# Row softmax on one core: the load of the fifth chunk issued as two DMAs of eight rows

## Chip, core and metric

The kernel runs on one core of one Trainium2 chip. The metric is the device time of one execution in microseconds (us). The kernel before took 161.8 us, the median of 3 runs (161.76 to 161.93). The profiled execution spans 160.5 us from its first to its last instruction.

## The reference

The input is an array of 16 x 1024 rows of 512 float32 numbers, 33.55 MB; the output has the same shape. Each row goes through a softmax with temperature 0.5:

```python
temp = 0.5
x_scaled = x / temp
x_max = np.max(x_scaled, axis=-1, keepdims=True)
exp_x = np.exp(x_scaled - x_max)
return (exp_x / np.sum(exp_x, axis=-1, keepdims=True)).astype(np.float32)
```

Every number is read once and written once, so 67.1 MB pass through the DMA engines.

## The kernel before, in words

The 16,384 rows are cut into C = 8 chunks of 2,048 rows. In a chunk each of the 128 partitions holds G = 16 rows that lie next to each other in DRAM, so a partition's share of a chunk is one contiguous run of 32 KiB, and a chunk is 4 MiB. `xt` is the tile of a chunk; there are `BUFS = 6` of them. Chunks 0 to 5 have a buffer each; chunk 6 takes the buffer of chunk 0 and chunk 7 that of chunk 1, so their loads must wait until the stores of chunks 0 and 1 are done. Everything happens in place: the exponentials and the scaled results overwrite the input in `xt`.

Three lists say how the work is cut. `LOADS` (L38) lists, for each chunk, the row ranges of its load DMAs: chunk 0 in two (rows 0 to 4 and 4 to 16), chunks 1 to 6 whole, chunk 7 without its last row. `BLOCKS` (L39) lists the row ranges for the computation: chunk 0 in three blocks, chunks 1 to 6 in one block, chunk 7 in two, 11 blocks in all. `STORES` (L40) stores each chunk whole, after its last block.

For a block `i` these steps are taken:

- `shift(i)`: if the chunk's load has not been issued yet, `load` issues it on SyncE's DMA queue (L68, queue q1 in the profile). VectorE takes the negated maximum of each row (L77, `negmax`) and doubles it (L81, `bias`).
- `exponentials(i)`: ScalarE computes exp(2x + bias) a row at a time and sums the row in the same instruction (L108).
- `scale_vector(i)`: VectorE takes the reciprocals of the sums (L125) and multiplies seven eighths of the rows by them (L127).
- `scale_scalar(i)`: ScalarE multiplies the other rows (L138).
- `store(i)`: ScalarE issues the store (L148, queue q10).

The order on each engine is written out by hand: the loop at the end of the kernel does, for each `i`, the exponentials of block `i + 1`, the scaling of block `i`, the maximum of block `i + 2` and the store of block `i`. VectorE thus alternates between the maximum of one chunk and the scaling of the one two before it. SyncE issues the loads of chunks 0 to 5 in the first microseconds, and they stand in its queue one behind the other.

The last row of each partition's share of chunk 7 goes another way: `load_last_row` issues it on GpSimd's queue (L97, q0) once ScalarE is at row 10 of chunk 5. A list named `finished` collects DMAs and last instructions for which SyncE waits at the very end (L174).

Of the kernel before, what the change touches and what calls it, by code (L numbers as in the profile page):

```python
# [1 line left out]

# [4 lines left out]


@with_exitstack
def kernel(  # L10
    ctx: ExitStack,
    tc: tile.TileContext,
    x: bass.AP,
    out: bass.AP,
):
    nc = tc.nc
    fp32 = mybir.dt.float32
    P = nc.NUM_PARTITIONS
    AX = mybir.AxisListType.X
    EXP = mybir.ActivationFunctionType.Exp  # L20
    COPY = mybir.ActivationFunctionType.Copy
    MAX = mybir.AluOpType.max

    D = x.shape[-1]
    xf = x.flatten_outer_dims()
    of = out.flatten_outer_dims()
    N = xf.shape[0]

    G = 16
    C = N // (P * G)
    assert C * P * G == N
    xr = xf.rearrange("(c p g) d -> c p g d", p=P, g=G)
    outr = of.rearrange("(c p g) d -> c p g d", p=P, g=G)
    WHOLE = [(0, G)]
    LOADS = [[(0, 4), (4, G)]] + [WHOLE] * 6 + [[(0, G - 1)]]  # L38
    BLOCKS = [[(0, 4), (4, 8), (8, G)]] + [WHOLE] * 6 + [[(0, 8), (8, G)]]  # L39
    STORES = [WHOLE] * 8  # L40
    BMAX = 16
    BUFS = 6

    data = ctx.enter_context(tc.tile_pool(name="data", bufs=BUFS))
    stats = ctx.enter_context(tc.tile_pool(name="stats", bufs=6))

    ctx.enter_context(tc.manual_schedule())


    warm = stats.tile([P, 1], fp32, name="warm", bufs=1)  # L50
    nc.vector.memset(warm, 0.0)  # L51
    nc.scalar.activation(out=warm, in_=warm, func=EXP)  # L52

    chunks = {}
    blocks = [(c, lo, hi) for c in range(C) for lo, hi in BLOCKS[c]]
    n = len(blocks)
    biases, sums, recips = {}, {}, {}

    finished = []

    def load(c):
        if c < BUFS:
            chunks[c] = data.tile([P, G, D], fp32, name="xt")
        else:
            chunks[c] = chunks[c - BUFS]
        xt = chunks[c]
        for lo, hi in LOADS[c]:
            part = nc.sync.dma_start(out=xt[:, lo:hi, :], in_=xr[c][:, lo:hi, :])  # L68
            finished.append(part.ins.name)

    def shift(i):
        c, lo, hi = blocks[i]
        if c not in chunks:
            load(c)
        b = hi - lo
        negmax = stats.tile([P, BMAX], fp32, name="negmax")
        nc.vector.tensor_reduce(  # L77
            negmax[:, 0:b], chunks[c][:, lo:hi, :], axis=AX, op=MAX, negate=True
        )
        biases[i] = stats.tile([P, BMAX], fp32, name="bias")  # L80
        nc.vector.tensor_scalar_mul(biases[i][:, 0:b], negmax[:, 0:b], 2.0)  # L81

    def load_last_row(signal):
        seen = stats.tile([P, 1], fp32, name="seen", bufs=1)
        copied = nc.gpsimd.tensor_copy(out=seen, in_=signal)  # L90
        finished.append(copied.ins.name)
        c = C - 1
        halves = "p (h d) -> p h d"
        to = chunks[c - BUFS][:, G - 1, :].rearrange(halves, h=2)
        of_ = xr[c][:, G - 1, :].rearrange(halves, h=2)
        for p0, p1 in ((P - 2, P), (0, P - 2)):
            part = nc.gpsimd.dma_start(  # L97
                out=to[p0:p1], in_=of_[p0:p1], max_dma_last_dim=2 * D
            )
            finished.append(part.ins.name)  # L100

    def exponentials(i, rows):
        c, lo, hi = blocks[i]
        if i not in sums:
            sums[i] = stats.tile([P, BMAX], fp32, name="sums")
        for g in rows:
            row = chunks[c][:, lo + g, :]
            nc.scalar.activation(  # L108
                out=row,
                in_=row,  # L110
                func=EXP,
                bias=biases[i][:, g : g + 1],
                scale=2.0,
                accum_out=sums[i][:, g : g + 1],
            )
            if c == BUFS - 1 and g == 10:
                load_last_row(sums[i][:, g : g + 1])


    def scale_vector(i):  # L120
        c, lo, hi = blocks[i]
        b = hi - lo
        k = b - b // 8
        recips[i] = stats.tile([P, BMAX], fp32, name="recip")
        nc.vector.reciprocal(recips[i][:, 0:b], sums[i][:, 0:b])  # L125
        rows = chunks[c][:, lo : lo + k, :]
        last = nc.vector.tensor_mul(  # L127
            rows, rows, recips[i][:, 0:k].unsqueeze(2).broadcast_to((P, k, D))
        )
        if i == n - 1:  # L130
            finished.append(last.ins.name)

    def scale_scalar(i):
        c, lo, hi = blocks[i]
        b = hi - lo
        for g in range(b - b // 8, b):
            row = chunks[c][:, lo + g, :]
            last = nc.scalar.activation(  # L138
                out=row, in_=row, func=COPY, scale=recips[i][:, g : g + 1]
            )  # L140
            if i == n - 1:
                finished.append(last.ins.name)

    def store(i):
        c, _, end = blocks[i]
        for lo, hi in STORES[c]:
            if hi == end:
                part = nc.scalar.dma_start(  # L148
                    out=outr[c][:, lo:hi, :], in_=chunks[c][:, lo:hi, :]
                )  # L150
                if c < C - 1:
                    finished.append(part.ins.name)

    shift(0)
    shift(1)

    def rows(i):
        c, lo, hi = blocks[i]
        cut = hi - lo - (2 if c == 1 else 0)
        return range(cut), range(cut, hi - lo)  # L160

    exponentials(0, rows(0)[0])
    for i in range(n):
        if i + 1 < n:
            exponentials(i + 1, rows(i + 1)[0])
        scale_vector(i)
        scale_scalar(i)
        if i + 2 < n:
            shift(i + 2)
        store(i)  # L170
        if i + 1 < n:
            exponentials(i + 1, rows(i + 1)[1])

    seen = nc.sync.nop()  # L174
    info = mybir.DependencyInfo(
        mybir.DependencyClass.Sync, mybir.DependencyReason.DATA
    )
    for name in finished:
        tc.add_manual_dep(seen.ins, name, info, reason="leaves one wait for the end")


# [1 line left out]
_INS = ['x']  # L183
_OUTS = [((16, 1024, 512), 'float32')]


# [23 lines left out]
```

## Time and profile before

| What | Number |
|---|---|
| time, median of 3 | 161.8 us |
| span of the profiled execution | 160.5 us |
| VectorE (DVE) busy | 134.6 us, 84% |
| ScalarE (ACT) busy | 102.2 us, 64% |
| DMA | 67.13 MB, mean 418 GB/s |
| maxima on VectorE (L77) | 11, together 69.9 us |
| scaling on VectorE (L127) | 11, together 62.0 us |
| exponentials on ScalarE (L108) | 128, together 90.4 us |
| stores (L148) | 8 of 4,096 KB, median 23.1 us from issue to landing |

A profile line of part 2 cuts the span into 40 slices of 4.0 us; each digit is the busy share of a slice in tenths. In part 3 a line gives a DMA queue, its packets, its MB and the share of the time of the 16 DMA engines that its packets took. A group of instructions reads: line, engine, operation, output and input, count, then busy time and the mean of one in ns, then the idle time ahead of them with what ended most of it. In a list of waits the numbers are total, count and longest. A line of DMA issues ends with the time from issue to landing. In a list by time the first number is the start, the second the duration.

A "piece" below is the contiguous run of one partition in one DMA, which the trace records as one packet: 32 KiB for a whole chunk.

### The profile page before, as it was taken

How to read it: one execution, taken by the hardware profiler on the slowest of the kernel's cores; microseconds unless marked ns; L12 is line 12 of the kernel's file. 1: busy time of each engine (PE TensorE's matmuls, PEld its weight loads, DVE VectorE, ACT ScalarE, POOL GpSimd, SP SyncE). 2: the span in 40 equal slices, each digit the busy share in tenths (PEclk: the TensorE clock that was granted, in tenths of full speed). 3: DMA queues.
4: the chain of work that ended last, by engine and by line, in shares of the span. 5: the costliest groups of instructions: out<-in, count | busy, mean ns of one | idle time of the engine just before them, and what ended most of it. 6: DMA issues, size and time to landing. Idle time of an engine off the chain costs nothing.

```text
span 160.5 us, 411 instructions
## 1 busy us (share of the span) xinstructions
DVE 134.6 (84%) x45; ACT 102.2 (64%) x273; POOL 1.9 (1%) x7
## 2 busy tenths in 40 slices
DVE  0607999999999999999999999999999999957000
ACT  3071549069989963998199909991899891790000
POOL 0000000000000000000000000030000000000000
DMA  5999999999989999999999999989999999999994
GB/s 184 470 408 498 400 392 457 457 392 402 506 269 425 490 392 400 506 400 392 490 425 392 474 434 392 490 383 483 422 450 400 400 465 441 392 457 449 400 441 204
DMA packets 2578, 67.13 MB, mean 418 GB/s; under 512 B 328, under 2 KB 328, under 8 KB 400
## 3 DMA queue, kind: packets, MB, share of 16 engines
q1 hardware_dynamic: 1296, 33.29, 49.3%
q10 hardware_dynamic: 1152, 33.55, 48.4%
q0 software_dynamic: 128, 0.26, 0.4%
q14 instruction: 2, 0.02, 0.0%
HBM read 33.55 MB, written 33.55 MB: 418 GB/s over the span
## 4 chain that ended last, share of the span: by engine, by line
DVE 75%; DMA 7%; issue 5%; ACT 3%; SPq 0%
DVE negmax L77 42%; DVE xt L127 31%; DMA xt<-in_x_dram 7%; ACT xt L108 3%; DVE bias L81 1%; DVE recip L125 1%; SPq L68 0%
## 5 line engine op out<-in xcount | busy, mean ns | idle before, releaser
L108 ACT ACTIVATE xt<-xt,bias 128x512 f32<-128x512 f32 x128 | 90.4, 708 | 41.5 <-DVE bias L81 40.6
L77 DVE TENSOR_REDUCE negmax<-xt 128x16 f32<-128x8192 f32 (+2 forms) x11 | 69.9, 6352 | 9.4 <-DMA xt<-in_x_dram 9.4
L127 DVE TENSOR_TENSOR xt<-xt,recip 128x7168 f32<-128x7168 f32 (+2 forms) x11 | 62.0, 5637 | 0.4
L108 ACT ACTIVATION_READ_ACCUMULATOR xt<-xt,bias 128x1 f32 x128 | 23.9, 187 | 0.0
L138 ACT ACTIVATE xt<-xt,recip 128x512 f32<-128x512 f32 x15 | 9.9, 706 | 0.0
L125 DVE RECIPROCAL recip<-sums 128x16 f32<-128x16 f32 (+2 forms) x11 | 2.4, 218 | 1.8 <-ACT xt L108 1.8
L81 DVE TENSOR_SCALAR bias<-negmax 128x16 f32<-128x16 f32 (+2 forms) x11 | 1.9, 173 | 0.4
L52 ACT ACT_TABLE_LOAD x1 | 1.3, 1283 | 0.7 <-PEq L194 0.7
L97 POOL DMA_DIRECT2D xt<-in_x_dram x2 | 1.5, 741 | 0.5 <-issue 0.5
L90 POOL COPY seen<-sums 128x1 f32<-128x1 f32 x1 | 0.2, 184 | 103.6 <-ACT xt L108 103.6
L51 DVE MEMSET warm<- 128x1 f32 x1 | 0.1, 59 | 0.8 <-PEq L194 0.8
L52 ACT ACTIVATE warm<-warm 128x1 f32<-128x1 f32 x1 | 0.2, 202 | 0.0
L194 POOL MEMSET const-float32-0.0<- 128x1 f32 x1 | 0.1, 93 | 0.2 <-issue 0.2
L194 POOL MEMSET const-bfloat16-1.0<- 128x1 bf16 x1 | 0.1, 95 | 0.0
L194 POOL MEMSET const-uint8-127<- 128x1 uint8 x1 | 0.1, 95 | 0.0
L194 POOL MEMSET const-float32-1.0<- 128x1 f32 x1 | 0.1, 93 | 0.0
## 6 DMA issues: line engine op xcount, KB each, us to landing
out_dram<-xt ACTq DMA_DIRECT2D x8, 4096.0 KB, 23.1
xt<-in_x_dram SPq DMA_DIRECT2D x6, 4096.0 KB, 34.8
xt<-in_x_dram SPq DMA_DIRECT2D x1, 3840.0 KB, 27.8
xt<-in_x_dram SPq DMA_DIRECT2D x1, 3072.0 KB, 11.6
xt<-in_x_dram SPq DMA_DIRECT2D x1, 1024.0 KB, 4.8
xt<-in_x_dram POOLq DMA_DIRECT2D x1, 252.0 KB, 15.4
xt<-in_x_dram POOLq DMA_DIRECT2D x1, 4.0 KB, 9.1
```

The source lines that it names most:

```text
L51: nc.vector.memset(warm, 0.0)
L52: nc.scalar.activation(out=warm, in_=warm, func=EXP)
L77: nc.vector.tensor_reduce(negmax[:, 0:b], chunks[c][:, lo:hi, :], axis=AX, op=MAX, negate=True)
L81: nc.vector.tensor_scalar_mul(biases[i][:, 0:b], negmax[:, 0:b], 2.0)
L90: copied = nc.gpsimd.tensor_copy(out=seen, in_=signal)
L97: part = nc.gpsimd.dma_start(out=to[p0:p1], in_=of_[p0:p1], max_dma_last_dim=2 * D)
L108: nc.scalar.activation(out=row, in_=row, func=EXP, bias=biases[i][:, g : g + 1], scale=2.0, accum_out=sums[i][:, g : g + 1],)
L125: nc.vector.reciprocal(recips[i][:, 0:b], sums[i][:, 0:b])
L127: last = nc.vector.tensor_mul(rows, rows, recips[i][:, 0:k].unsqueeze(2).broadcast_to((P, k, D)))
L138: last = nc.scalar.activation(out=row, in_=row, func=COPY, scale=recips[i][:, g : g + 1])
L194: nc = _bacc.Bacc("TRN2", target_bir_lowering=False, num_devices=1)
```

## The change

The load of the fifth chunk (index 4) is issued as two DMAs of eight rows each, one behind the other on the same queue. The pieces are then 16 KiB instead of 32 KiB. Each DMA has its own semaphore; the maximum of that chunk is still taken over all sixteen rows and so waits for both. Blocks and stores stay as they are.

The change is for the share of the DMA engines that loads and stores get: the fifth chunk is the one whose load is in progress when the first store is issued. It sets the size of the pieces in which that load is cut.

```diff
     WHOLE = [(0, G)]
     LOADS = [[(0, 4), (4, G)]] + [WHOLE] * 6 + [[(0, G - 1)]]
+    LOADS[4] = [(0, 8), (8, G)]
     BLOCKS = [[(0, 4), (4, 8), (8, G)]] + [WHOLE] * 6 + [[(0, 8), (8, G)]]
     STORES = [WHOLE] * 8
```

## The prediction

> **What bounds the kernel now.** I read first the 40 slices and the queues, then the groups by line with their waits, then the VectorE rows in order of time near the end, and last the DMA issues one by one.
>
> ```profile
> DVE  0607999999999999999999999999999999957000
> DMA  5999999999989999999999999989999999999994
> q1 hardware_dynamic: 1296, 33.29, 49.3%
> q10 hardware_dynamic: 1152, 33.55, 48.4%
> ```
>
> Two things are full together. The DMA engines are busy from the second slice to the last: loads (q1, issued by SyncE) take 49.3% of their time, stores (q10, issued by ScalarE) 48.4%, together 98%. VectorE is full from 12.8 to about 140 us. Stores start only in slice 12; from there to about 115 us loads and stores share the 16 engines; after that only stores are left.
>
> ```profile
> L77 DVE TENSOR_REDUCE negmax<-xt 128x16 f32<-128x8192 f32 (+2 forms) x11 | 69.9, 6352 | 9.4 <-DMA xt<-in_x_dram 9.4
> L127 DVE TENSOR_TENSOR xt<-xt,recip 128x7168 f32<-128x7168 f32 (+2 forms) x11 | 62.0, 5637 | 0.4
> ...
> DVE negmax L77 <- DMA xt<-in_x_dram: 9.4, 2, 4.8
> ```
>
> VectorE waits for a load twice only, both for the first chunk (until 5.5 and 12.8 us). Every later load, the fifth included, lands before its maximum is wanted. How much before is what the change spends, so I list landings (issue plus time to landing) against the starts of the maxima.
>
> ```profile
> xt<-in_x_dram SPq DMA_DIRECT2D x1, 4096.0 KB, 73.0
> xt<-in_x_dram SPq DMA_DIRECT2D x1, 4096.0 KB, 27.6
> xt<-in_x_dram SPq DMA_DIRECT2D x1, 3840.0 KB, 27.8
> ...
> 87.24 8.68 DVE L77 TENSOR_REDUCE negmax<-xt 128x16 f32<-128x8192 f32 x1
> 103.86 8.68 DVE L77 TENSOR_REDUCE negmax<-xt 128x16 f32<-128x8192 f32 x1
> 120.48 4.41 DVE L77 TENSOR_REDUCE negmax<-xt 128x8 f32<-128x4096 f32 x1
> 147.48 0.34 ACTq L148 DMA_DIRECT2D out_dram<-xt  x1
> out_dram<-xt ACTq DMA_DIRECT2D x1, 4096.0 KB, 12.2
> ```
>
> The three loads are the sixth chunk (issued 3.9), the seventh (68.7) and the eighth (88.0). They land at 76.9, 96.3 and 115.8; the maxima start at 87.2, 103.9 and 120.5. The margins shrink: 10.3, 7.6, 4.7 us. The reason is that a load and a store of 4 MiB, sharing the engines, take 19.4 us, while VectorE takes 16.6 us a chunk (87.24 to 103.86).
>
> At the end both limits meet. The last store is issued at 147.48, and its first packet starts at 148.47; the engines end their last packet of the store before between 148.3 and 149.5, then need eight packets each, 9.70 us, to 159.2. So DMA sets the end, and VectorE has about 1.0 us of slack (149.5 less 148.47).
>
> **What the Trainium skill says.** "DMA: Bandwidth & Descriptors", section "Queues, rings and completion order": each DMA engine goes round-robin over the queues that have work, at packet granularity. The trace agrees: while the sixth chunk loads (56.9 to 75.4) there are 138 records of each queue. And size doesn't matter: 252 KB of the last row, in pieces of 4 KiB and less, take 15.4 us from issue to landing beside 32 KiB pieces, which a share by bytes would not give. Same page, "Issuing engines are not separate DMA queues": all queues run on the same 16 engines; the sum of 98% agrees. "Perfetto Trace Analysis", section "DMA Optimizations": splitting DMAs helps if the engines are generally idle. Here they are not.
>
> **The change, part by part.**
>
> *Removed and added.* One load of 128 pieces of 32 KiB becomes two of 128 pieces of 16 KiB; the rows of one partition are adjacent in DRAM. Between 6.0 and 11.4 us 96 pieces of 24 KiB take 101.3% of 16 engines: 0.912 us each. Between 148.6 and 158 us 127 pieces of 32 KiB take 102.5%: 1.214 us. The 8 KiB between them cost 0.302 us, so a piece has some 0.006 us beside its bytes, and 16 KiB costs 0.610 us. Two instead of one, eight times an engine: 8 x 0.006, and 16 more semaphore records of 0.009 us, one an engine: together 0.06 us. DMA being full, that counts in full if nothing else moves.
>
> *Issue and waits.* SyncE issues one more DMA, 0.4 us, at about 3.5 us. In the built program the sixth chunk's load now also waits until the first load has landed (5.5 us), since it takes over its semaphore; behind it stand only the loads of chunks seven and eight, which wait for stores until 68.7 and 88.0. The sixth chunk's data start to move at 56.9, so both are hidden under the loads before. VectorE waits on two semaphores for the fifth chunk instead of one (the load lands at 57.5, the maximum starts at 70.6), and ScalarE gets one wait more amid its exponentials: nothing, since both have long come.
>
> *What moves.* The fifth load is under way when the first store begins. It starts at about 41.5; up to 48.4 each engine starts 5 of its 8 pieces, up to 49.9 almost one more, and from there 33 pieces in all, 2.1 an engine, go turn about with store pieces. One turn then is 0.61 + 1.21 us instead of 2 x 1.21, and each smaller piece lets one whole store piece by. So the load lands later, by 1.21 us for each store piece let by in excess, and the loads behind it on q1 as well; the stores come earlier by as much.
>
> How many pieces are left when the store comes in is not shown. The store is issued at 44.10 and enters about 1.0 us later (the first load: issued 0.74, first packets 1.7). After that an engine still starts two load pieces, and in that time all engines lose some 1.1 us once (pieces that start at about 46.3 take 2.3 to 2.5 us). If these two are a count of pieces, the store gets its turn at 45.1 + 0.3 + 2 x 0.61 + 1.1 = 47.7 us; the load has then moved for 47.7 - 41.5 - 1.1 = 5.1 us, 8.4 of 16 pieces, and 7.6 are left, 5.5 more than now. If they stand for an amount of bytes, the turn comes as now and 4.1 pieces are left, 2 more. Lower end 2 x 1.21 = 2.4 us, upper end 5.5 x 1.21 = 6.7 us. I take 5 pieces, 6.1 us: queues are served by the piece, and I expect work in flight to be held so too.
>
> *Where it arrives.* Sixth chunk 76.9 + 6.1 = 83.0 (wanted 87.2), seventh 96.3 + 6.1 = 102.4 (wanted 103.9): hidden. Eighth 115.8 + 6.1 = 121.9, wanted 120.5: VectorE waits 1.4 us. Behind that wait on VectorE are the seventh chunk's scaling and the last maximum, for which ScalarE's last eight exponentials wait, then the last scaling and the last store. VectorE waits for nothing else between 120.5 and 143, and the 1.8 us that it waits for ScalarE before L125 come after the last maximum and move with it. So the store is issued at 147.48 + 1.4 = 148.9, its first packet starts at 149.9, and 9.70 us follow: 159.6, against 159.2. The engines then are empty and start one after the other (15 pieces of the very first load started between 1.7 and 2.3 us), which adds between 0 and 0.6. Sum: +0.4 to +1.0 us, taken +0.6: 161.8 + 0.6 = 162.4 us. The 0.06 us from above lie under the wait.
>
> **The rivals.**
>
> *No change (161.9).* The pieces in flight count by bytes, or fewer stores get by: the delay is 2.4 us, the eighth load lands at 118.2, in time; even a wait of up to 1.0 us is covered by the slack at the end, that is a delay of up to 5.7 us. Then +0.06 us remain. For it: my 6.1 is only just over 5.7. Against: the trace has 1:1 turns at any size.
>
> *Faster (161.3).* The 1.1 us that all engines lose when the first store enters shrink with the load piece in flight, to 0.55 us. Since DMA sets the end, 0.55 us come off; VectorE's slack of 1.0 us allows it, if the eighth load is in time. For it: the loss falls on load pieces alone, never again later. Against: it can as well be a cost of the first store itself.
>
> *Slower still (163.1).* The delay is 6.7 us, and the last row's small pieces, now turning about with the eighth load, add about 0.4: VectorE waits 2.4 us, the store is issued at 149.9, its packets start at 150.9, 1.4 us after the engines are free: +1.4. Near my upper end; I count it as a part of "slower".
>
> **How the numbers follow.** Forecast, slower by 0.6 us, 0.42; slower still 0.07; no change 0.33; faster 0.18. The bound of 0.2% is 0.3 us. Range: the low end takes in no change and most of the faster case, 161.4; the high end is the upper end of the delay, 163.1. Left out is about a tenth on the fast side and less on the slow one.
>
> **What would show it.** Right: q10 gains on q1 between 47 and 62 us; the first store lands near 63 us instead of 68.6; the seventh load lands near 102 us; the maximum of the eighth chunk waits for its load by about 1.4 us, a third DMA wait in the list of waits; the last store is issued near 148.9 and still takes about 12 us. Wrong: no third wait, and the last store still issued at 147.5; then it was the bytes in flight. A faster kernel would show load pieces without the long records at 46 us. What would upset it altogether: turns that are not one piece each, so that two small pieces go in one turn.

## The result and the profile after

| | before | after |
|---|---|---|
| time, median | 161.86 us (161.75 to 162.08, 6 runs) | 162.93 us (162.58 to 163.62, 6 runs) |
| ratio, 95% interval | | 1.0069 [1.0046, 1.0093] |

The kernel became slower by 1.07 us, 0.7%. Run again (first experiment) it was slower by 0.55 us. The profiled execution after is the slowest of its six runs; the profile of before that stands ahead of the prediction was itself slower than all six timed runs above (162.29 us; a second one, below, has 161.84 us and a span of 160.1).

The page of the changed kernel, parts 2, 3 and 4: the slices of the DMA engines, the GB/s, the queue of the loads, and the chain that ended last, by engine.

```profile
DMA  5999999999899999999999999999999999999992
GB/s 183 466 438 471 389 446 462 389 446 456 377 341 402 454 430 462 389 438 462 398 446 462 389 446 448 411 465 391 442 433 454 414 430 454 414 430 446 414 438 89
q1 hardware_dynamic: 1440, 33.29, 48.9%
DMA 45%; DVE 29%; ACT 11%; issue 6%; SPq 0%
```

The load queue has 144 records more: 128 pieces and 16 semaphore records. The DMA engines are as full as before, until the last slice: there they move 89 GB/s, where it was 204. Most engines are done there; the end, below, shows that one is not. And the chain that ended last now runs through DMA for 45% of the span; before it was VectorE for 75%.

Next, VectorE's waits for loads, and the issues with their landings: the sixth chunk (issued 5.6), the seventh (66.1), the eighth (85.5) and the first store (44.2); then the two moments that the prediction was about.

```profile
DVE negmax L78 <- DMA xt<-in_x_dram: 9.7, 3, 4.8
...
xt<-in_x_dram SPq DMA_DIRECT2D x1, 4096.0 KB, 76.3
xt<-in_x_dram SPq DMA_DIRECT2D x1, 4096.0 KB, 35.9
xt<-in_x_dram SPq DMA_DIRECT2D x1, 3840.0 KB, 35.3
out_dram<-xt ACTq DMA_DIRECT2D x1, 4096.0 KB, 21.8
...
120.86 4.42 DVE L78 TENSOR_REDUCE negmax<-xt 128x8 f32<-128x4096 f32 x1 [0.23 <-DMA xt<-in_x_dram]
147.88 0.34 ACTq L149 DMA_DIRECT2D out_dram<-xt  x1
```

The loads land at 81.9, 102.0 and 120.8 us, 5.0 to 5.7 us later than before; the first store lands at 66.0, 2.6 earlier. The third wait of VectorE is there, but it is 0.23 us. The last store is issued 0.4 us later than before.

The next view counts the pieces while the fifth load and the first store share the engines, 49 to 58 us after the change: queue, records, MB, share of 16 engines.

```profile
q10 hardware_dynamic: 78, 2.56, 65.7%
q1 hardware_dynamic: 80, 1.31, 34.0%
```

Turns go by the piece: 80 pieces of 16 KiB against 78 of 32 KiB, so the loads get a third of the engines' time. Five pieces an engine of the fifth load are left at 49 us, where there were two large ones (2.2 in the profile before, 2.1 in that of experiment 5).

The end, in stretches: start and end in us, length, busy time of VectorE, ScalarE and GpSimd, granted clock, share of DMA, and GB/s of what was started. 82 GB/s over 0.4 us is one piece of 32 KiB.

```profile
158.00:158.40 0.40, 0.00 (x0) 0.00 (x0) 0.00 (x0) 1.00 0.19 82
158.40:158.80 0.40, 0.00 (x0) 0.00 (x0) 0.00 (x0) 1.00 0.01 0
158.80:159.20 0.40, 0.00 (x0) 0.00 (x0) 0.00 (x0) 1.00 0.20 82
```

After 158 us two pieces start, one behind the other: one DMA engine is a piece behind the rest. Fifteen engines end the last store by 159.28 us, half of them by 158.84; the sixteenth ends at 160.40, and it sets the span.

### The profile page after: what moved, and what is told of

Read it like the earlier page. It is cut to its first block, busy times and chain, and to the rows that moved or that the text cites. A ratio compares the mean times of both kernels' runs of the same rounds, so it can differ in the third digit from the quotient of the medians.

```text
span 161.6 us, 413 instructions
## 1 busy us (share of the span) xinstructions
DVE 134.7 (83%) x45; ACT 102.4 (63%) x273; POOL 1.9 (1%) x7
## 4 chain that ended last, share of the span: by engine, by line
DMA 45%; DVE 29%; ACT 11%; issue 6%; SPq 0%
DMA xt<-in_x_dram 29%; DVE negmax L78 20%; DMA out_dram<-xt 16%; ACT xt L109 10%; DVE xt L128 8%; ACT xt L139 1%; DVE bias L82 1%; DVE recip L126 0%; SPq L69 0%
## 5 line engine op out<-in xcount | busy, mean ns | idle before, releaser
L109 ACT ACTIVATION_READ_ACCUMULATOR xt<-xt,bias 128x1 f32 x128 | 25.0, 195 | 0.0
```

The source lines that it names most:

```text
L109: nc.scalar.activation(out=row, in_=row, func=EXP, bias=biases[i][:, g : g + 1], scale=2.0, accum_out=sums[i][:, g : g + 1],)
```

## Experiments

In the diffs, minus is the kernel before or the changed kernel, as said. "Outside the span" is the time of the profiled run less its span.

**1. The changed kernel again, unedited.**

> The changed kernel once more, for a second profile. Theory A (the late eighth load makes VectorE wait, so the last store is issued late): VectorE's wait for the eighth load is 0.3 to 1.5 us and the last store's first packet starts as much later than 148.5 us; all 16 DMA engines then end within some 0.5 us of each other. Theory B (one DMA engine falls behind the others by about a store piece while loads and stores take turns, and that engine ends last): most engines end by about 159.2 us as in the kernel before, one ends 1 to 1.5 us after them, whatever VectorE does. Time about 162.9 us under both.

Measured: 162.41 us (six of seven runs 162.37 to 162.57, the profiled one 163.46), ratio 1.0045 [1.0027, 1.0062]. The same picture in the profile: VectorE's maximum of the eighth chunk starts 0.2 us late, the last store is issued at 147.71, fifteen engines end by 159.28, one at 160.21. The windows of this run read as above:

```profile
158.00:158.40 0.40, 0.00 (x0) 0.00 (x0) 0.00 (x0) 1.00 0.19 82
158.40:158.80 0.40, 0.00 (x0) 0.00 (x0) 0.00 (x0) 1.00 0.01 0
158.80:159.20 0.40, 0.00 (x0) 0.00 (x0) 0.00 (x0) 1.00 0.20 82
```

Theory B holds for the two long runs that were profiled. It isn't all of the slowdown: the other six runs here are still over the kernel before by 0.5 to 0.7 us. Whether an engine lags in them isn't shown, as none was profiled.

**2. The fourth load cut instead of the fifth** (against the change):

```diff
-    LOADS[4] = [(0, 8), (8, G)]
+    LOADS[3] = [(0, 8), (8, G)]
```

> The fourth chunk's load is cut in two instead of the fifth's. That load is over before the first store begins, so small pieces meet no store pieces. Theory A and theory B: no change, 161.9 us, plus at most 0.1 us for 128 more pieces. If cutting a load costs by itself (issue, semaphores, waits, per-piece time), it is as slow as the change, 162.9 us.

Measured: 162.16 us, ratio 1.0020 [1.0012, 1.0027]: 0.3 us slower, while VectorE's waits are those of before and the span of the profiled run is 160.03 us, no longer than before (160.06 in experiment 5).

```profile
DVE negmax L78 <- DMA xt<-in_x_dram: 9.4, 2, 4.8
```

So cutting a load costs 0.3 us that lies outside the span, where no small piece meets a store; the rest of the slowdown needs the meeting. That 0.3 us was in neither theory.

**3. The sixth load cut instead of the fifth** (against the change):

```diff
-    LOADS[4] = [(0, 8), (8, G)]
+    LOADS[5] = [(0, 8), (8, G)]
```

> The sixth chunk's load is cut in two instead of the fifth's. All of that load takes turns with stores, so each engine lets 8 more store pieces by, 9.7 us. Theory A with its turns of one piece each: the sixth load lands at 86.6, the seventh at 106.0, the eighth at 125.5 us; VectorE waits 2 us for the seventh and 5 us in all, the last store is issued near 152.5, time about 165.9 us. Theory B alone, without VectorE's wait: about 163 us, as after the change. If turns go by bytes: no change.

Measured: 166.34 us, ratio 1.0279 [1.0237, 1.0321]. From its waits and its order of time:

```profile
DVE negmax L78 <- DMA xt<-in_x_dram: 13.4, 4, 4.8
...
105.53 8.69 DVE L78 TENSOR_REDUCE negmax<-xt 128x16 f32<-128x8192 f32 x1 [1.67 <-DMA xt<-in_x_dram]
124.64 4.42 DVE L78 TENSOR_REDUCE negmax<-xt 128x8 f32<-128x4096 f32 x1 [2.39 <-DMA xt<-in_x_dram]
151.65 0.34 ACTq L149 DMA_DIRECT2D out_dram<-xt  x1
```

Here the predicted mechanism is at work in full: two new waits, 4.1 us in all (2 for the seventh load and 5 in all were expected), the last store 4 us late, and all engines end it together (162.23 to 162.40). With enough pieces in turns, VectorE's wait sets the end; in the change there were too few. The profile is of a run of 165.66 us; two of the six runs took over 168 us, and what they add isn't shown.

**4. The fifth load and the first store both in halves** (against the change):

```diff
-    STORES = [WHOLE] * 8
+    STORES = [[(0, 8), (8, G)]] + [WHOLE] * 7
...
-            if hi == end:
+            if end == G:
```

> The fifth load is cut in two as in the change, and the first store is cut in two as well, both halves issued where the whole was; so both queues have pieces of 16 KiB while they meet. Theory A: no extra store bytes get by, the eighth load lands as before the change (115.8 us), VectorE doesn't wait, 161.9 us. Theory B: if the unequal pieces put one engine out of step, it is gone too; if the cut load itself does it, 162.9 us stay.

Measured: 162.45 us, ratio 1.0043 [1.0030, 1.0056]. The first half of the store went out at 39.8 us, 4.2 us ahead of the second, since its rows don't wait for ScalarE's last row; so it isn't quite the experiment that was meant. VectorE doesn't wait, and no engine falls behind (158.98 us against 158.86 for the next). Both are as expected for equal pieces. The time, though, is that of the first experiment's shorter runs: the lag of one engine and the time outside the span are two things. Outside it are 2.17 us here, against 1.78 for the kernel before. When the first store enters, an engine loses 0.94 us (the records between 39 and 52 us, less the usual time of such a piece): less than the 1.16 to 1.19 us of the change, though the load's pieces are as small.

**5. The kernel before again.**

> The kernel before, once more, for a second profile and to see how time and span stand to each other. All theories: 161.9 us, span about 160.1 us in an undisturbed run, time 1.8 us above the span; no DMA engine ends more than 0.3 us behind the others.

Measured: 161.84 us, ratio 1.0001 [0.9993, 1.0010]; span of the profiled run 160.06, outside it 1.78. Half of the engines end the last store by 158.41 us, the last at 158.86. No piece starts after 158 us:

```profile
158.00:158.40 0.40, 0.00 (x0) 0.00 (x0) 0.00 (x0) 1.00 0.01 0
158.40:158.80 0.40, 0.00 (x0) 0.00 (x0) 0.00 (x0) 1.00 0.01 0
```

**6. One more instruction on SyncE, no other DMA** (against the kernel before):

```diff
             finished.append(part.ins.name)
+        if c == 5:
+            extra = nc.sync.nop()
+            for name in (finished[0], finished[2], finished[3]):
+                tc.add_manual_dep(extra.ins, name, info, reason="one more wait on SyncE")
```

(`info` stands for the dependency record that the kernel's last lines also use.)

> The kernel before with one more instruction on SyncE (three more waits ahead of the seventh load, on loads that have long landed), and no other DMA. Theory C (the cut load's kernels have a SyncE program one instruction longer, which brings one more 8 KiB block of instructions to load before the first instruction; the time outside the span rises by 0.27 us): 162.15 us at an unchanged span of 160.1 us. If the extra time outside the span comes from the additional DMA itself: 161.9 us.

Measured: 161.79 us, ratio 0.9995 [0.9987, 1.0004]; outside the span 1.78. Theory C falls. In this profile, too, one engine is behind, by 0.4 us (159.33 against 158.92), and the run is the longest of its thirteen (162.31).

**7. VectorE about 1 us late** (against the kernel before; the memset is extra work, nothing is left out):

```diff
+    idle = stats.tile([P, 960], fp32, name="idle", bufs=1)
...
         b = hi - lo
+        if i == n - 2:
+            nc.vector.memset(idle, 0.0)
```

> The kernel before with about 1 us of idle work (a memset of a tile that nobody reads) on VectorE just ahead of the eighth chunk's first maximum. Theory A as in the prediction (slack of 1.0 us at the end): last store issued near 148.5, no change or up to 0.4 us slower, 161.9 to 162.3 us. If there is no slack: 162.9 us. So a wait of 0.2 to 0.3 us, as both profiles of the changed kernel have it, would cost nothing under the first and 0.3 us under the second.

```profile
120.67 0.86 DVE L78 MEMSET idle<- 128x960 f32 x1
121.45 4.36 DVE L80 TENSOR_REDUCE negmax<-xt 128x8 f32<-128x4096 f32 x1
148.39 0.34 ACTq L151 DMA_DIRECT2D out_dram<-xt  x1
```

Measured: 162.44 us, ratio 1.0036 [1.0023, 1.0049]. The last store goes out 0.77 us later than in experiment 5 (147.62), the span is 160.33: 0.27 us longer. So about 0.5 us of VectorE's lateness were free here, and 0.2 to 0.3 us, as the change causes, should cost nothing; experiment 10 has the change without any such wait. But the time rose by 0.6 us: outside the span are 2.06 us again. This kernel has no additional DMA and no additional semaphore; it has one more instruction on VectorE. So has every kernel with 2.05 us or more outside its span: where the fifth, fourth or sixth load is cut, VectorE waits on two semaphores, and the trace has one more semaphore instruction on VectorE than before.

**8. A tiny store at the start** (against the kernel before; the numbers stored are overwritten by the first real store):

```diff
+    first = nc.scalar.dma_start(out=outr[0][:, 0, 0:1], in_=warm)
     nc.scalar.activation(out=warm, in_=warm, func=EXP)
...
-    finished = []
+    finished = [first.ins.name]
```

> The kernel before with a store of one number per partition on ScalarE's queue at the very start (rows that the first real store overwrites later). If the 1.1 us that all engines lose when the first store enters belong to the first use of the store queue, they move to the start: the pieces at 46 us keep to 1.21 us each and the DMA engines are done up to 1 us earlier, about 161.0 us. If they belong to the first large store among loads: unchanged, 161.9 us, or 162.1 with a longer program.

Measured: 162.16 us, ratio 1.0017 [1.0009, 1.0025]. The loss at the first large store stays: the records between 44 and 52 us, less their usual 1.213 us each, sum to 0.93 us an engine. It isn't the first use of the queue. Two load pieces there took 2.96 and 2.99 us, and at the end two engines are behind by 0.6 us (159.47 and 159.50, the next 158.84). That suggests that what an engine loses at 47 us it still lacks at the end; that they are the same two engines the trace doesn't say. Outside the span are 1.78 us, so the 0.3 us by which this kernel is slower lie in the span.

**9. VectorE's program longer, nothing else** (against the kernel before):

```diff
     nc.vector.memset(warm, 0.0)
+    more = stats.tile([P, 1], fp32, name="more", bufs=1)
+    nc.vector.memset(more, 0.0)
```

> The kernel before with one more memset of a single number per partition at the start of VectorE's program, where VectorE waits for the first load anyway (about 0.06 us of work, hidden). Theory D (VectorE's program, one instruction longer, costs 0.28 us outside the span; all kernels with the longer program have 2.05 to 2.15 us between span and time, the others 1.74 to 1.81): 162.13 us at an unchanged span of 160.1 us. Otherwise: 161.85 us.

Measured: 162.11 us, ratio 1.0014 [1.0008, 1.0021], span 159.97, outside it 2.06 us. Theory D holds: one instruction that does nothing on the path costs 0.25 us, none of it in the span of the profiled run.

**10. The changed kernel with VectorE's program as long as before** (against the change):

```diff
-    nc.vector.memset(warm, 0.0)
+    nc.gpsimd.memset(warm, 0.0)
```

> The changed kernel, with the memset of the warm-up tile given to GpSimd, so that VectorE's program is as long as before the change. Theory D: time outside the span falls from 2.05 to about 1.77 us, the time by 0.28 us, to about 162.15 us on a chip where the change takes 162.4. What is left over the kernel before, 0.3 us or more, lies in the span: theory B, one DMA engine that ends about 1 us after the others in a disturbed run, some 0.3 us otherwise. If theory D is wrong: 162.4 us.

Measured: 162.42 us, ratio 1.0035 [1.0022, 1.0048]. Outside the span are 1.78 us, as the theory has it; the time is above the expected 162.15 because the span of the profiled run is 160.57, half a microsecond over that of before. VectorE waits for no load but the first here (the eighth chunk's maximum starts at 120.44), so this half microsecond is DMA alone: half of the engines end the last store by 158.84 us (158.41 in experiment 5), the last one at 159.38.

```profile
120.44 4.41 DVE L78 TENSOR_REDUCE negmax<-xt 128x8 f32<-128x4096 f32 x1
147.44 0.34 ACTq L149 DMA_DIRECT2D out_dram<-xt  x1
```

The last store goes out 0.2 us earlier than in experiment 5 (147.62), and the kernel is slower all the same. The median equals that of experiment 1, though 0.28 us outside the span are gone: the time in the span differs that much from one set of runs to another.

**11. The same edit in the kernel before** (GpSimd clears the warm-up tile).

> The kernel before with the same memset given to GpSimd, so that VectorE's program is one instruction shorter than before. Control of the edit itself. Theory D with a threshold just above the program of before: 161.85 us. If each instruction costs: 161.6 us.

Measured: 161.94 us, ratio 1.0002 [0.9995, 1.0010]; outside the span 1.78. One instruction fewer gains nothing, so it isn't a price for each instruction. The two kernels with two more on VectorE (experiments 4 and 12) have 2.17 and 2.18 us outside, 0.1 above those with one more.

**12. The fifth load in four** (against the change):

```diff
-    LOADS[4] = [(0, 8), (8, G)]
+    LOADS[4] = [(0, 4), (4, 8), (8, 12), (12, G)]
```

> The fifth chunk's load in four DMAs of four rows, pieces of 8 KiB. Turn model as corrected by the profiles (the first store enters a fixed time after its issue, at about 49 us, whatever the piece size; from there one store piece a load piece): about 5 of 16 rows are left then, so 10 small pieces where the change has 5, and 5 more store pieces get by than after the change, 6 us. Most engines then end the eighth load at 117.3 + 6.1 = 123.4 us, VectorE waits for it by 3 to 4 us, the last store is issued near 151 and the span is about 163 us; with 0.3 to 0.4 us more outside the span for two or more added instructions on VectorE the time is about 165.2 us. If turns went by bytes: 162.5 to 163 us, as after the change. If the loss at the first store grows again with smaller pieces (0.8 us at 32 KiB, 1.17 at 16 KiB): about 1.5 us of it.

```profile
122.21 4.42 DVE L78 TENSOR_REDUCE negmax<-xt 128x8 f32<-128x4096 f32 x1 [1.70 <-DMA xt<-in_x_dram]
149.22 0.34 ACTq L149 DMA_DIRECT2D out_dram<-xt  x1
...
158.40:158.80 0.40, 0.00 (x0) 0.00 (x0) 0.00 (x0) 1.00 3.05 1311
```

Measured: 162.93 us, ratio 1.0065 [1.0051, 1.0079]. VectorE waits 1.7 us, not 3 to 4. Ten small pieces an engine were left at 50 us, but the first store has only eight pieces an engine, and all of them had started by 62.1 us, when the fifth load ended; the second store, issued at 58.9, came too late to take more turns. Half of the engines end the eighth load by 120.0 us where the change has 117.2: 2.8 us, about two store pieces, not five. In the last line 16 pieces start within 0.4 us (1311 GB/s): the engines end together, because all had waited for VectorE's late store. The loss at the first store is 1.17 us, as with 16 KiB.

## Why the prediction was right, and where not

The direction, the range and the turns by the piece were right. The way from there to the end was not: the wait of VectorE, which was to make up the whole +0.6 us, cost nothing that the runs show, and three things that the prediction put at nothing took its place. That the measured time still lies in the range is in good part luck. By the prediction's own signs it was between right and wrong: there is a third wait, but of 0.23 us, and the last store is issued at 147.9; in experiment 10 there is none and the store goes out at 147.4, which was to mean that bytes in flight count, yet the kernel is slower.

| Step of the prediction | Said | Measured |
|---|---|---|
| price of a 16 KiB piece | 0.610 us | 0.61 us |
| pieces left when the store enters | 7.6, taken 5 more store pieces let by | 5 left, 3 more let by |
| landing of sixth, seventh, eighth load | 83.0, 102.4, 121.9 | 81.9, 102.0, 120.8 |
| landing of the first store | near 63 | 66.0 |
| VectorE's slack at the end | 1.0 us | about 0.5 (experiment 7) |
| VectorE's wait for the eighth | 1.4 us | 0.23 us; 0.2 in the second profile, none in the third |
| last store issued | 148.9 | 147.9 |
| VectorE's second semaphore wait | nothing | 0.28 us outside the span |
| one-off loss at the first store | 1.1, may shrink to 0.55 | 1.16 to 1.19, against 0.65 to 1.00 (once 1.09) |
| all engines end together | taken for granted | one ends 0.9 to 1.1 us after the next in two profiles, 0.35 in a third |

*The turns.* The 138 records of each queue, from which the prediction read one piece in turn, contain 10 and 16 semaphore records; the pieces are 128 and 122. The reading holds.

*The pieces left.* The step "enters about 1.0 us later, after that an engine still starts two load pieces" failed. From issue to the first store piece it is 4.3 us before and 4.6 us after, and 3.8 to 4.6 us in the experiments, with no order by the size of the load pieces. So the pieces left were near the prediction's lower case. Half of the engines ended the eighth load by 117.2 instead of 113.5: 3.7 us, three store pieces (4.4 us against experiment 5, which has 112.8 and the smaller loss). The landing of 120.8 came close to the forecast for another reason: it is the one late engine, 2.9 us behind the next (semaphore records at 117.56 and 120.44). In the kernel before, one engine lands last as well (115.23, the next 113.29, in experiment 5), but by 1.9 us. Had the engine kept to that, the load would have come about a microsecond earlier and VectorE wouldn't have waited.

*The slack.* "VectorE has about 1.0 us of slack" was of the right kind and too large: experiment 7 puts it at about 0.5 us. It was read from a profile in which the DMA engines were later than usual: the last of them was free for the last store at 149.5, against 149.18 in experiment 5, where that store's first piece starts at 148.46. A wait of 0.2 to 0.3 us, as in the change, is covered either way. Experiments 3 and 12 show the predicted wait in earnest, with 4.1 and 1.7 us. In the rival "no change" it was this step that was right.

*What the 1.07 us are.* The parts are read from single profiles, the 1.07 us from medians. First, 0.28 us outside the span, by the longer VectorE program: the six profiled runs with 1.78 us outside (before, experiments 5, 6, 8, 10, 11) all have a VectorE program no longer than before, the eight with 2.05 or more (after, experiments 1 to 4, 7, 9, 12) all have a longer one, and experiment 9 shows it alone.

Second, about 0.35 us in the span, as the loss at the first store is larger: 1.16 to 1.19 us an engine in the three profiles with the fifth load in 16 KiB and the store in 32, against 0.65 to 1.00, on the mean 0.82, in eight with it whole (experiments 2, 3, 5 to 9, 11); the profile of before ahead of the prediction had 1.09, the one exception. The ends of the median engine agree: 158.78 to 158.84 us against 158.26 to 158.46 (experiments 2, 5, 6, 8, 9, 11), and the exception's 158.93. Together they make 0.63 us, about what the shorter runs of experiment 1 show (0.5 to 0.7); the first six runs of the change are over the kernel before by 0.7 us or more.

Third, the lag of one engine, up to 1.1 us: it is in the profiles of two of the three longest runs of the change (163.3 to 163.6, of thirteen; the third has no profile), and no run of the kernel before took more than 162.41. How much of the remaining 0.4 us of the median is this lag isn't shown. No experiment takes the second or the third alone away: that they come from the cut is read from the profiles side by side.

*The rival "faster"* was wrong in its premise: beside store pieces of 32 KiB the loss is larger, not smaller, with load pieces of 16 KiB, and no larger again with 8 KiB (1.17 us). With both in 16 KiB it was 0.94 us (experiment 4), within what whole loads show; there the store also came earlier, so that the size of the load's pieces alone sets the loss isn't shown.

What stays open is why the loss is larger, and what puts one engine so far behind. One engine is 0.4 to 0.9 us behind the median one at 42 us in every profile: at about 37.5 us a block of 8 KiB of instructions is fetched, 0.31 us, and in all profiles but the first the piece beside it takes some 0.36 us more. After the change another long piece or two follow between 60 and 74 us (0.63 us over at 64.0; 0.36 at 64.0 in experiment 1, 0.73 at 72.4 in experiment 10). But experiment 6, with the fifth load whole, has one too (0.48 at 91.0) and one engine 0.4 us behind, while experiment 4, with small pieces, has no long piece there and no lag at the end. That it is the same engine each time the trace doesn't say, since it doesn't name the engine of a record. No kernel here beat the kernel before.

## What to carry to other kernels

Where loads and stores keep the DMA engines full, as here, the size of a load's pieces sets its share: the queue with smaller pieces got one of them for each piece of the other. So before a load is cut, ask what waits for it and for those behind it. Before a wait is priced by its length, compare it with the slack at the end, in more than one profile, and ask whether all DMA engines end together. And compare time with span: an edit that only adds a semaphore to wait for cost 0.3 us here that no view of the span shows.

## What the runs showed of the hardware

- A VectorE program one instruction longer raised the time outside the span from 1.78 to 2.06 us (experiments 7 and 9), one two longer to 2.17 and 2.18 (experiments 4 and 12); one shorter changed nothing (experiment 11), and neither did one more on SyncE (experiment 6) or on ScalarE (experiment 8).
- The first store's pieces start 3.8 to 4.6 us after its issue when the engines are full of loads, at load pieces of 32, 16 and 8 KiB alike. Where the engines have run empty by the time of the last store (experiments 3, 7 and 12), its pieces start 0.84 to 1.0 us after its issue.
- On the way the engines lose 0.65 to 1.19 us on the mean, once (with the fifth load whole or in small pieces), and unequally: in experiment 8 two pieces take some 1.2 us longer than those beside them at 47 us, and two engines end 0.6 us after the others.
- "DMA: Bandwidth & Descriptors" in the Trainium skill (section "Queues, rings and completion order") has a typical turn at 9 to 17 descriptors; here a turn is one record of 8, 16 or 32 KiB. How many descriptors such a record has the trace doesn't say.
